# Same-chunk products of a gated scan, 64 x 64 in two column halves of the matmul array instead of 128 x 128

## The chip, the cores and the metric

The kernel runs on one core of a Trainium2 chip. The metric is the device time of one execution in microseconds (us). Besides it, a trace of one profiled execution is used; it shows every instruction of the five engines: TensorE (PE in the rows; its weight loads are PEld), VectorE (DVE), ScalarE (ACT), GpSimd (POOL) and SyncE (SP, which issues DMAs).

## What is computed

The reference is a two-layer backbone over 640 tokens (128 context tokens and 512 latent ones) of width 1024. A layer multiplies the modulated tokens by one wide input matrix, feeds four mixers (HGRN2, neighbourhood attention, MLA, short convolution), gates and projects their outputs, and ends in a layer norm. The change touches the HGRN2 mixer alone: four heads per layer, each a gated linear scan, forwards and backwards, in chunks.

```python
def step(S, inp):                       # one chunk
    qc, kc, vc, gc = inp
    b = jnp.cumsum(gc, axis=2)
    diff = b[:, :, :, None, :] - b[:, :, None, :, :]
    decay = jnp.exp(jnp.where(causal[:, :, None], diff, -jnp.inf))
    attn = jnp.einsum('bhtd,bhsd,bhtsd->bhts', qc, kc, decay)
    o = (jnp.einsum('bhts,bhse->bhte', attn, vc)
         + jnp.einsum('bhtd,bhde->bhte', qc * jnp.exp(b), S))
    ...
o_f, s_f = chunk_gla(q, heads(k_f, HG_DK), v, heads(lg_f, HG_DK), s0_f)
o_b, s_b = chunk_gla(rev(q), rev(heads(k_b, HG_DK)), rev(v), rev(heads(lg_b, HG_DK)), s0_b)
```

`attn` is the product of a query and a key under the decay between their positions. Every (query, key) pair has its own decay, so `attn` is not one plain matmul.

## The kernel before, in words

**The large work.** The input matrix comes as 128-column chunks. `zchunk` (line 237) takes one chunk's weights, which `take_w` (line 163) loads by DMA and splits in a high part `whi` (a cast on ACT, line 160) and a low part `wlo` (a subtraction on DVE, line 161), and multiplies them with the tokens' high and low parts in `zmm` (line 211): three matmuls for each of eight 128-row slices, for 384 tokens, and again for 256. These are the matmuls of line 217. The merges and the output use `mm3` (line 200, matmuls of line 208).

**The order of the work.** Each mixer is a generator. `tick` (line 141), called once before each half of a `zchunk`, lets every active generator go on by one step when its wait has run out. `hg_mix` (line 483) yields `HG_WAIT = 2` before each of its matmul groups, so about one group of HGRN matmuls stands between two halves of the large work. Within that, a scheduler orders each engine's instructions from the written order and from priorities; `take_w` asks for its load and split 300 places early. Each engine then runs its queue strictly in that order.

**The HGRN head.** `hg_mix` has the 640 tokens as five blocks `j` of 128. `RK` holds two copies of the keys, `RQ` two copies of the queries (forward and backward scan), channels on partitions. The products `A` (640 columns: for each `j`, 128 keys on partitions by 128 queries) are built in eight steps:

- the self product (line 501): five f32 matmuls of 128 keys by 128 queries, copied to `A` by ACT (line 503);
- seven levels, `B` = 1, 2, 4, ... 64. A level is the product of keys in one run of `B` positions with queries in the neighbouring run. ACT gathers the keys to `km` (line 511); five matmuls (line 516) read the queries through an access pattern that takes `B` elements from one copy of `RQ` and `B` from the other in turn; DVE writes the result to `A` where the level's mask is set (`copy_predicated`, line 519); then DVE multiplies the gates into `RK` and `RQ` for the next level (lines 524, 526, 528) and halves the gate products (line 530).

Most of what a level computes is masked away. Afterwards `A` is multiplied with the values (line 572), together with the states (lines 549, 562).

One f32 matmul of the program is two pairs of weight load (LDWEIGHTS) and MATMUL in the trace, so a group of five shows as x10. I call such a group a burst. Two layers of four heads with eight bursts each make 64.

Of the kernel before, what the change touches and what calls it, by code (L numbers as in the profile page):

```python
# [11 lines left out]
U8 = mybir.dt.uint8  # L12
# [6 lines left out]
T = 640  # L19
# [63 lines left out]
def ap_of(t, off, dims):  # L83
    base = t[:]
    return bass.AP(tensor=base.tensor, offset=base.offset + off, ap=[list(base.ap[0])] + [list(d) for d in dims])


class Build:
# [216 lines left out]

    def setup_tables(self):
        nc, I, cp = self.nc, self.I, self.cp
        mk = self.s([128, 7, 128])
        nc.scalar.dma_start(mk, I["masks"])
        self.masks = cp.tile([128, 7, 128], U8, name="masks")  # L310
        nc.vector.tensor_copy(self.masks, mk)
        self.cs = cp.tile([128, 2, 512], F32, name="cs")
        nc.scalar.dma_start(self.cs, I["cs"])
# [169 lines left out]
    def hg_mix(self, l, h, z, out):  # L483
        nc = self.nc
        G, RK, RQ, q, vT, sg = z
        S0 = self.u([128, 2, 128])
        nc.sync.dma_start(S0, self.I["S0"][l, h])
        ks = self.t()
        nc.vector.tensor_tensor(ks, RK[:, 0, :], RK[:, 1, :], ALU.add)
        yield HG_W0  # L490

        ps = self.mx()
        for j in range(5):
            nc.tensor.transpose(ps[:, j * 128:(j + 1) * 128], vT[:, j * 128:(j + 1) * 128], self.ident)
        v = self.t()
        nc.scalar.copy(v, ps[:, :T])

        ps = self.mx()
        for j in range(5):
            sl = slice(j * 128, (j + 1) * 128)  # L500
            nc.tensor.matmul(ps[:, sl], ks[:, sl], q[:, sl], start=True, stop=True)
        A = self.t()
        nc.scalar.copy(A, ps[:, :T])
        nc.vector.tensor_tensor(RQ[:, 0, :], q, G[:, 0, :], ALU.mult)
        nc.vector.tensor_tensor(RQ[:, 1, :], q, G[:, 1, :], ALU.mult)
        Tb, n = G, T
        for lev in range(7):
            B = 1 << lev
            np_ = T // (2 * B)
            km = self.t()  # L510
            nc.scalar.copy(km.rearrange("p (n u b) -> p n u b", u=2, b=B),
                           ap_of(RK, 0, [[2 * B, np_], [T + B, 2], [1, B]]))
            yield HG_WAIT
            ps = self.mx()
            for j in range(5):
                nc.tensor.matmul(ps[:, j * 128:(j + 1) * 128], km[:, j * 128:(j + 1) * 128],  # L516
                                 ap_of(RQ, j * 128, [[2 * B, 64 // B], [T + B, 2], [1, B]]),
                                 start=True, stop=True)
            nc.vector.copy_predicated(A.rearrange("p (j t) -> p j t", j=5),  # L519
                                      self.masks[:, lev:lev + 1, :].to_broadcast([128, 5, 128]),  # L520
                                      ps[:, :T].rearrange("p (j t) -> p j t", j=5))

            kf = ap_of(RK, 0, [[2 * B, np_], [1, B]])
            nc.vector.tensor_tensor(kf, kf, ap_of(Tb, n + 1, [[2, np_], [0, B]]), ALU.mult)
            kb = ap_of(RK, T + B, [[2 * B, np_], [1, B]])
            nc.vector.tensor_tensor(kb, kb, ap_of(Tb, 0, [[2, np_], [0, B]]), ALU.mult)
            rq = ap_of(RQ, 0, [[2 * B, np_], [T + B, 2], [1, B]])
            nc.vector.tensor_tensor(rq, rq, ap_of(Tb, 1, [[2, np_], [n - 1, 2], [0, B]]), ALU.mult)  # L528
            T2 = self.t([128, 2, np_]) if lev == 0 else self.u([128, 2, np_])
            nc.vector.tensor_tensor(T2, ap_of(Tb, 0, [[n, 2], [2, np_]]), ap_of(Tb, 1, [[n, 2], [2, np_]]), ALU.mult)  # L530
            Tb, n = T2, np_
        yield HG_WAIT

        order = ((0, 1, 2, 3), (0, 4, 3, 2))
        ps = self.mx()
        for d in range(2):
            for i, j in enumerate(order[d]):
                o = (4 * d + i) * 128
                nc.tensor.transpose(ps[:, o:o + 128], RK[:, d, j * 128:(j + 1) * 128], self.ident)
        kt = [self.t([128, 4, 128]) for _ in range(2)]  # L540
        for d in range(2):
            nc.scalar.copy(kt[d], ps[:, 512 * d:512 * d + 512].rearrange("p (i t) -> p i t", i=4))
        yield HG_WAIT
        vv = lambda j: v[:, j * 128:(j + 1) * 128]
        ps = self.mx()
        for d in range(2):
            for i, j in enumerate(order[d]):
                o = (4 * d + i) * 128
                nc.tensor.matmul(ps[:, o:o + 128], kt[d][:, i, :], vv(j), start=True, stop=True)  # L549
        st = self.u([128, 2, 128])  # L550
        nc.scalar.copy(st, ps.rearrange("p (d i t) -> p d i t", d=2, i=4)[:, :, 0, :])
        nc.sync.dma_start(self.O["state"][l, h], st)
        S = [self.u([128, 3, 128]) for _ in range(2)]
        terms = {j: [(A[:, j * 128:(j + 1) * 128], vv(j))] for j in range(5)}
        for d in range(2):
            prev = S0[:, d, :]
            for i in range(1, 5):
                j = order[d][i] if i < 4 else (4, 1)[d]
                terms[j].append((RQ[:, 1 - d, j * 128:(j + 1) * 128], prev))
                if i < 4:  # L560
                    o = (4 * d + i) * 128
                    nc.vector.scalar_tensor_tensor(S[d][:, i - 1, :], prev, Tb[:, 1 - d, j:j + 1], ps[:, o:o + 128],
                                                   ALU.mult, ALU.add)
                    prev = S[d][:, i - 1, :]
        yield HG_WAIT

        ps = self.mx()
        for j in range(5):
            if j == 3:
                yield 1  # L570
            for i, (a, b) in enumerate(terms[j]):
                nc.tensor.matmul(ps[:, j * 128:(j + 1) * 128], a, b, start=(i == 0), stop=(i == len(terms[j]) - 1))  # L572
        sq = self.t()
        nc.scalar.activation(sq, ps[:, :T], AF.Square)
        ss = self.sm([128, 5])
        nc.vector.tensor_reduce(ss, sq.rearrange("p (j e) -> p j e", j=5), AX.X, ALU.add)
        r = self.sm([128, 5])
        self.rsqrt(r, ss, 5, 1.0 / 128, EPS)
        on = sq
        nc.vector.tensor_tensor(on.rearrange("p (j e) -> p j e", j=5), ps[:, :T].rearrange("p (j e) -> p j e", j=5),  # L580
                                r.unsqueeze(2).to_broadcast([128, 5, 128]), ALU.mult)
        yield HG_WAIT
        ps = self.mx()
        for j in range(5):
            nc.tensor.transpose(ps[:, j * 128:(j + 1) * 128], on[:, j * 128:(j + 1) * 128], self.ident)
        nc.vector.scalar_tensor_tensor(sg, ps[:, :T], self.vec("normg", l), sg, ALU.mult, ALU.mult)
        out[h] = sg
# [478 lines left out]
    def out_norm(self, l, p):  # L1066
# [12 lines left out]
        for c in range(8):  # L1079
# [4 lines left out]
            if l + 1 < L:  # L1084
                for o, x, j in ((0, 128, 0), (128, n, 1)) if p == 0 else ((0, n, 1),):
                    A, B = self.hA[:, c, j:j + 1], self.hB[:, c, j:j + 1]
                    nc.scalar.activation(self.h_hi[:, c, a + o:a + x], y[:, o:x], AF.Identity, bias=B, scale=A)
                    if p == 0 and F_POOL:
                        nc.gpsimd.tensor_scalar(f[:, o:x], y[:, o:x], A, B, ALU.mult, ALU.add)
                    elif p == 1 and F_ACT:  # L1090
# [215 lines left out]
def _consts():  # L1306
    c = {}
    c["ident"] = np.eye(128, dtype=np.float32)
    s = np.arange(128)
    masks = np.zeros((128, 7, 128), np.float32)  # L1310
    for i in range(7):
        B = 1 << i
        blk = s // B
        same = (blk[:, None] // 2) == (blk[None, :] // 2)
        masks[:, i, :] = same & (blk[:, None] != blk[None, :])
    c["masks"] = masks
    t = np.arange(512)
    row, col = (t // 64).astype(np.float32), (t % 64).astype(np.float32)
    inv = (np.float32(1.0) / (np.float32(10000.0) ** (np.arange(16, dtype=np.float32) / np.float32(16)))).astype(np.float32)
    ang = np.concatenate([row[:, None] * inv, col[:, None] * inv], axis=-1).astype(np.float32)  # L1320
    cos, sin = np.cos(ang).astype(np.float32).T, np.sin(ang).astype(np.float32).T
    c["cs"] = np.stack([np.concatenate([cos] * 4, axis=0), np.concatenate([sin, -sin] * 2, axis=0)], axis=1)
    return c
# [90 lines left out]
```

## Time and profile before

| | |
|---|---|
| median of 3 runs | 2148.61 us (2146.55 to 2150.0) |
| the profiled execution, its own time | 2149.83 us |
| its span, first to last instruction | 2148.0 us |
| TensorE matmul, busy | 2095.0 us, 98% |
| VectorE, busy | 1378.0 us, 64% |
| ScalarE, busy | 867.1 us, 40% |
| granted TensorE clock, mean | 0.989 |

Busy times count an instruction from its start to its end, and on TensorE neighbouring instructions overlap: a matmul of 0.33 us can be followed by the next after 0.17 us. What a matmul takes away from its engine is therefore read from the distance between two starts, not from its own duration. A bracket at the end of a timeline row gives the idle time of the engine before it, and who ended it. The page's "chain" follows the work that ended last back to what released it.

### The profile page before, as it was taken

To read this page: it belongs to the slowest core of one execution; us is meant where nothing else is said; L and a number is where in the kernel's file an instruction comes from. 1 tells how busy PE (TensorE), PEld (TensorE's weight loads), DVE (VectorE), ACT (ScalarE), POOL (GpSimd) and SP (SyncE) were. 2 spreads that over 40 slices of the span, in tenths; PEclk is the share of its full clock that TensorE was granted. 3 is DMA by queue.
4 is the path that set the end of the run, shared out by engine and by line. 5 is a ranking of instruction groups with operands and counts; after the bars stand their busy time and mean duration, and the time that the engine had idled before them with its cause. 6 is when DMAs were issued, how large, how long until landed. Compare 5 with 4: busy or idle time off the path is not lost.

```text
span 2148.0 us, 35645 instructions
## 1 busy us (share of the span) xinstructions
PE 2095.0 (98%) x14538; PEld 2055.4 (96%) x14538; DVE 1378.0 (64%) x2648; ACT 867.1 (40%) x1531; POOL 179.1 (8%) x156
## 2 busy tenths in 40 slices
PE   7999999999999999999999999999999999999997
PEld 4999999998999999999999999999999999999997
DVE  5677776657666467734587876875575546775456
ACT  4333233344444466523352323343343336653332
POOL 0000000221111023200010000012000002221000
PEclk9999999999999999999999999999999999999998
DMA  7221222242222221122432222233221221222251
GB/s 281 78 63 61 65 67 70 86 132 77 93 96 93 67 68 62 60 74 74 148 116 72 62 62 65 62 101 91 61 75 61 60 67 59 71 66 60 75 166 50
DMA packets 70485, 178.05 MB, mean 83 GB/s; under 512 B 7985, under 2 KB 20913, under 8 KB 70321
## 3 DMA queue, kind: packets, MB, share of 16 engines
q1 hardware_dynamic: 67440, 169.32, 24.9%
q10 hardware_dynamic: 2880, 6.45, 0.9%
q8 instruction: 114, 1.87, 0.4%
q14 instruction: 51, 0.41, 0.1%
HBM read 168.20 MB, written 7.54 MB: 82 GB/s over the span
## 4 chain that ended last, share of the span: by engine, by line
PE 87%; DVE 7%; issue 2%; ACT 2%; DMA 2%; POOL 0%; SPq 0%; DVEq 0%; ACTq 0%; POOLq 0%
PE g L217 55%; PE g L208 13%; PE mx L516 3%; PE mx L756 2%; PE mx L971 2%; PE mx L208 1%; PE mx L794 1%; PE mx L217 1%; DVE wlo L161 1%; PE mx L938 1%; PE mx L572 1%; DVE t L161 1%; PE mx L770 1%; PE mx L549 1%; PE mx L394 1%
## 5 line engine op out<-in xcount | busy, mean ns | idle before, releaser
L217 PE MATMUL g<-h_hi,whi 128*128 128x256 f32 (+1 forms) x2880 | 905.2, 315 | 10.7 <-DVE e L1024 6.9
L217 PE MATMUL g<-h_lo,whi 128*128 128x256 f32 (+1 forms) x2880 | 893.5, 310 | 2.2 <-DVE h_lo L412 2.1
L217 PE MATMUL g<-h_hi,wlo 128*128 128x256 f32 (+1 forms) x2880 | 892.9, 310 | 0.6 <-DVE wlo L161 0.6
L217 PEld LDWEIGHTS g<-h_hi,whi 128*128 128x128 f32 x2880 | 548.1, 190 | 14.7 <-DVE e L1024 8.0
L217 PEld LDWEIGHTS g<-h_lo,whi 128*128 128x128 f32 x2880 | 549.0, 191 | 3.7 <-DVE h_lo L412 2.7
L217 PEld LDWEIGHTS g<-h_hi,wlo 128*128 128x128 f32 x2880 | 548.5, 190 | 1.0 <-DVE wlo L161 1.0
L161 DVE TENSOR_TENSOR wlo<-wraw,whi 128x1024 fp32r<-128x1024 f32 (+1 forms) x258 | 285.1, 1105 | 279.6 <-ACT whi L160 277.9
L160 ACT CAST whi<-wraw 128x1024 fp32r<-128x1024 f32 (+1 forms) x258 | 242.5, 940 | 478.4 <-PE g L217 261.0
L208 PE MATMUL g<-t,whi 128*128 128x256 f32 (+1 forms) x1280 | 284.7, 312 | 4.9 <-ACT e L1009 4.9
L208 PEld LDWEIGHTS g<-t,whi 128*128 128x128 f32 x1280 | 215.3, 190 | 6.2 <-ACT e L1009 5.7
L208 PE MATMUL g<-t,wlo 128*128 128x384 f32 (+1 forms) x640 | 198.3, 310 | 0.0
L387 POOL TENSOR_TENSOR t<-t 128x512 f32<-128x512 f32 x56 | 79.7, 1423 | 1017.0 <-ACT t L386 1016.0
L894 POOL TENSOR_SCALAR u<-u,sm 128x320 f32<-128x320 f32 (+2 forms) x80 | 89.9, 1135 | 569.7 <-DVE sm L892 532.9
L208 PEld LDWEIGHTS g<-t,wlo 128*128 128x128 f32 x640 | 121.5, 190 | 0.0
L1009 ACT ACTIVATE e<-g,hbin 128x384 f32<-128x384 f32 (+1 forms) x128 | 66.9, 523 | 116.0 <-PE g L217 115.9
L516 PE MATMUL mx<-s,t 128*128 128x128 f32 x560 | 76.4, 285 | 4.1 <-DVE s L528 4.1
L260 ACT ACTIVATE e<-g,hbin 128x384 f32<-128x384 f32 x76 | 39.8, 524 | 98.0 <-PE g L217 80.8
L516 PEld LDWEIGHTS mx<-s,t 128*128 128x128 f32 x560 | 72.8, 192 | 4.4 <-issue 4.4
L261 DVE TENSOR_SCALAR e<-g,vecs 128x384 f32<-128x384 f32 x76 | 41.4, 544 | 48.6 <-ACT e L260 48.4
L457 DVE RECIPROCAL s<-e 128x384 f32<-128x384 f32 (+1 forms) x32 | 68.9, 2152 | 0.9
L385 DVE SCALAR_TENSOR_TENSOR t<-t,cf 128x512 f32<-128x512 f32 x56 | 51.8, 925 | 20.5 <-DMA t<-in_wada 20.2
L519 DVE COPY_PREDICATED t<-masks,mx 128x640 f32<-128x640 uint8 x56 | 49.0, 876 | 23.8 <-PE mx L516 23.8
(282 smaller groups left out, 2672.1 us busy)
## 6 DMA issues: line engine op xcount, KB each, us to landing
wraw<-in_win SPq DMA_DIRECT2D x184, 512.0 KB, 3.5
wraw<-in_wbr SPq DMA_DIRECT2D x64, 256.0 KB, 2.6
t<-in_wada SPq DMA_DIRECT2D x64, 256.0 KB, 4.2
wraw<-in_wout SPq DMA_DIRECT2D x20, 512.0 KB, 4.4
s<-in_wada SPq DMA_DIRECT2D x16, 512.0 KB, 7.6
s<-in_nabias SPq DMA_DIRECT2D x8, 640.0 KB, 4.7
m<-in_xT SPq DMA_DIRECT2D x8, 320.0 KB, 8.4
t<-in_xT ACTq DMA_DIRECT2D x8, 320.0 KB, 5.0
```

The source lines that it names most:

```text
L160: nc.scalar.copy(hi, raw)
L161: nc.vector.tensor_tensor(lo, raw, hi.bitcast(F32), ALU.subtract)
L208: nc.tensor.matmul(o, wsl(a, k), xsl(b, k, i), start=(k == 0 and p == 0), stop=(k == nk - 1 and p == 2))
L217: nc.tensor.matmul(ps[:, :e - a], at(u, k), v[:, k, a:e], start=(k == 0 and i == 0), stop=(k == 7 and i == 2))
L385: nc.vector.scalar_tensor_tensor(acc[0], raw, cf(0), acc[0], ALU.mult, ALU.add)
L387: nc.gpsimd.tensor_tensor(acc[1], acc[1], raw, ALU.add)
L457: nc.vector.reciprocal(g, r)
L516: nc.tensor.matmul(ps[:, j * 128:(j + 1) * 128], km[:, j * 128:(j + 1) * 128], ap_of(RQ, j * 128, [[2 * B, 64 // B], [T + B, 2], [1, B]]), ...
L519: nc.vector.copy_predicated(A.rearrange("p (j t) -> p j t", j=5), self.masks[:, lev:lev + 1, :].to_broadcast([128, 5, 128]), ps[:, :T].rea ...
L756: nc.tensor.matmul(ps[:, e * 512:e * 512 + NH], a, b[:, e * NH:(e + 1) * NH], start=(n == 0), stop=(n == 4))
L894: NORM(nc).tensor_scalar(p[e], p[e], sums[:, e:e + 1], None, ALU.mult)
L1009: self.zchunk(l, "merge", n * 8 + c, lambda ps, p, sl: nc.scalar.activation(th[p], ps, AF.Tanh, bias=hb, scale=0.5))
```

## The change

The HGRN head no longer multiplies 128 keys by 128 queries. For the self product and the levels `B` = 1 to 32 it takes the 64 keys and 64 queries of each half-block, and puts the result of the first half on the output partitions 0 to 63 and that of the second half on 64 to 127; by this the weights of the first half lie in the columns 0 to 63 of the array and those of the second in 64 to 127. For `B` = 64 the keys of one half meet the queries of the other half. All results are compact: 64 columns for each `j`, 320 in all, in a tile `C` instead of `A`. The mask shrinks to 6 levels of 64 columns. At the last level ACT copies `C` and the last result to the four quadrants of `A` (four copies of 64 x 5 x 64 each head); that level has no `copy_predicated` any more.

```diff
-        mk = self.s([128, 7, 128])
+        mk = self.s([128, 6, 64])
...
+        halves = (slice(0, 64), slice(64, 128))
+        five = lambda x: x[:, 0:320].rearrange("p (j t) -> p j t", j=5)
         ps = self.mx()
         for j in range(5):
-            sl = slice(j * 128, (j + 1) * 128)
-            nc.tensor.matmul(ps[:, sl], ks[:, sl], q[:, sl], start=True, stop=True)
-        A = self.t()
-        nc.scalar.copy(A, ps[:, :T])
+            for i, r in enumerate(halves):
+                sl = slice(j * 128 + 64 * i, j * 128 + 64 * i + 64)
+                nc.tensor.matmul(ps[r, j * 64:(j + 1) * 64], ks[:, sl], q[:, sl], start=True, stop=True)
+        C = self.t([128, 5, 64])
+        nc.scalar.copy(C, five(ps))
...
             for j in range(5):
-                nc.tensor.matmul(ps[:, j * 128:(j + 1) * 128], km[:, j * 128:(j + 1) * 128],
-                                 ap_of(RQ, j * 128, [[2 * B, 64 // B], [T + B, 2], [1, B]]),
-                                 start=True, stop=True)
-            nc.vector.copy_predicated(A.rearrange("p (j t) -> p j t", j=5),
-                                      self.masks[:, lev:lev + 1, :].to_broadcast([128, 5, 128]),
-                                      ps[:, :T].rearrange("p (j t) -> p j t", j=5))
+                for i, r in enumerate(halves):
+                    o = j * 128 + 64 * i
+                    if B < 64:
+                        x = ap_of(RQ, o, [[2 * B, 32 // B], [T + B, 2], [1, B]])
+                    else:
+                        x = RQ[:, 1 - i, j * 128 + 64 - 64 * i:j * 128 + 128 - 64 * i]
+                    nc.tensor.matmul(ps[r, j * 64:(j + 1) * 64], km[:, o:o + 64], x, start=True, stop=True)
+            if B < 64:
+                nc.vector.copy_predicated(C, self.masks[:, lev:lev + 1, :].to_broadcast([128, 5, 64]), five(ps))
+            else:
+                A = self.t()
+                Aj = A.rearrange("p (j t) -> p j t", j=5)
+                for i, r in enumerate(halves):
+                    nc.scalar.copy(Aj[r, :, 64 * i:64 * i + 64], C[r])
+                    nc.scalar.copy(Aj[r, :, 64 - 64 * i:128 - 64 * i], five(ps)[r])
```

In the changed file the self product is line 506, the level matmul 527, `copy_predicated` 529, the four copies 535 and 536; the lines 524, 526 and 528 of before are 539, 541 and 543, and line 1022 is 1037.

**An ordinary burst.** TensorE's queue at the first self product (line 501, now 506), between the 384-token half and the 256-token half of a chunk; `mx` and `g` are PSUM tiles, `t` a tile in SBUF. Before:

```order
L217 MATMUL g<-h_hi,whi 128x384
L217 MATMUL g<-h_lo,whi 128x384
L217 MATMUL g<-h_hi,wlo 128x384
L501 MATMUL mx<-t 128x128 x5
L217 MATMUL g<-h_hi,whi 128x256
```

After:

```order
L217 MATMUL g<-h_hi,whi 128x384
L217 MATMUL g<-h_lo,whi 128x384
L217 MATMUL g<-h_hi,wlo 128x384
L506 MATMUL mx<-t 64x64 x10
L217 MATMUL g<-h_hi,whi 128x256
```

The burst stays where it was, with twice the matmuls of a quarter the size. This holds for all bursts but one in each layer.

**The burst that moves.** TensorE's queue at level `B` = 16 of the fourth head, in the first merge (line 208 is the merge's matmul). Before, two of the five matmuls stand right behind the merge's matmuls and three follow after 24 rows of line 217:

```order
L208 MATMUL g<-t,whi 128x256 x2
L208 MATMUL g<-t,wlo 128x256
L516 MATMUL mx<-s,t 128x128 x2
L217 MATMUL g<-h_hi,whi 128x384
L217 MATMUL g<-h_lo,whi 128x384
```

After, all ten stand behind those 24 rows:

```order
L217 MATMUL g<-h_hi,whi 128x384
L217 MATMUL g<-h_lo,whi 128x384
L217 MATMUL g<-h_hi,wlo 128x384
L527 MATMUL mx<-s,t 64x64 x10
L217 MATMUL g<-h_hi,whi 128x256
```

**VectorE at the same place.** Line 385 is part of the next modulation's sum, 161 makes `wlo`, 519 (now 529) is the masked copy and 528 (now 543) the query update that the burst waits for. Before:

```order
L385 SCALAR_TENSOR_TENSOR t<-t,cf 128x512
L526 TENSOR_TENSOR s<-s,u 128x5x64
L385 SCALAR_TENSOR_TENSOR t<-t,cf 128x512 x2
L161 TENSOR_TENSOR wlo<-wraw,whi 128x1024
L519 COPY_PREDICATED t<-masks,mx 128x640
L528 TENSOR_TENSOR s<-s,u 128x40x2x8
L1022 SCALAR_TENSOR_TENSOR m<-e,g 128x384
```

After:

```order
L385 SCALAR_TENSOR_TENSOR t<-t,cf 128x512
L541 TENSOR_TENSOR s<-s,u 128x5x64
L385 SCALAR_TENSOR_TENSOR t<-t,cf 128x512
L529 COPY_PREDICATED t<-masks,mx 128x320
L543 TENSOR_TENSOR s<-s,u 128x40x2x8
L161 TENSOR_TENSOR wlo<-wraw,whi 128x1024
L1037 SCALAR_TENSOR_TENSOR m<-e,g 128x384
```

The masked copy and the query update now stand ahead of `wlo` and of one row of line 385.

## Rows read from the trace of the kernel before

**Rows 1.** The page, part 1: busy time, share of the span, instructions.

```profile
PE 2095.0 (98%) x14538; PEld 2055.4 (96%) x14538; DVE 1378.0 (64%) x2648; ACT 867.1 (40%) x1531; POOL 179.1 (8%) x156
```

**Rows 2.** The page, part 4: the chain that ended last, by engine.

```profile
PE 87%; DVE 7%; issue 2%; ACT 2%; DMA 2%; POOL 0%; SPq 0%; DVEq 0%; ACTq 0%; POOLq 0%
```

**Rows 3.** HGRN windows: length; busy PE, PEld, DVE, ACT, POOL; PEclk, DMA share, GB/s.

```profile
119.00:427.00 308.00, 304.68 (x2187) 304.04 (x2186) 222.52 (x377) 104.34 (x156) 10.86 (x7) 1.00 0.22 69
1170.00:1480.00 310.00, 306.67 (x2190) 306.00 (x2188) 230.84 (x397) 105.63 (x158) 10.87 (x7) 0.99 0.22 69
```

**Rows 4.** Groups by line and shape: count, busy us, mean ns, idle before.

```profile
L516 PE MATMUL mx<-s,t 128*128 128x128 f32 x560 | 76.4, 285 | 4.1 <-DVE s L528 4.1
L501 PE MATMUL mx<-t 128*128 128x128 f32 x80 | 10.2, 275 | 0.0
```

**Rows 5.** Timeline, weight loads around three bursts: start, us, engine, line.

```profile
128.08 1.69 PEld L516 LDWEIGHTS mx<-s,t 128*128 128x128 f32 x10
129.74 0.20 PEld L217 LDWEIGHTS g<-h_hi,whi 128*128 128x128 f32 x1
...
136.77 1.32 PEld L516 LDWEIGHTS mx<-s,t 128*128 128x128 f32 x10
138.02 0.19 PEld L217 LDWEIGHTS g<-h_hi,whi 128*128 128x128 f32 x1
...
144.83 0.19 PEld L217 LDWEIGHTS g<-h_hi,wlo 128*128 128x128 f32 x1
145.01 1.25 PEld L516 LDWEIGHTS mx<-s,t 128*128 128x128 f32 x10
146.18 0.19 PEld L217 LDWEIGHTS g<-h_hi,whi 128*128 128x128 f32 x1
```

**Rows 6.** Timeline, weight loads: full f32 weights, 2 moving columns each.

```profile
420.60 1.87 PEld L394 LDWEIGHTS mx<-ones,t 128*128 128x128 f32 x16
422.38 0.30 PEld L208 LDWEIGHTS g<-t,whi 128*128 128x128 f32 x2
```

**Rows 7.** Timeline, weight loads: four short pairs on one tile of the array.

```profile
18.13 0.32 PEld L359 LDWEIGHTS mx<-ident,t 4*128 4x128 f32 x4 [0.86 <-issue]
```

**Rows 8.** Timeline, weight loads: f32 matmuls over halves of the array's rows.

```profile
794.91 0.19 PEld L217 LDWEIGHTS g<-h_lo,whi 128*128 128x128 f32 x1
795.03 0.19 PEld L217 LDWEIGHTS g<-h_hi,wlo 128*128 128x128 f32 x1
795.35 0.30 PEld L903 LDWEIGHTS mx<-u,t 64*128 64x128 f32 x4
795.77 0.19 PEld L217 LDWEIGHTS g<-h_hi,whi 128*128 128x128 f32 x1
```

**Rows 9.** Timeline, weight loads: to and from matmuls with 4 weight columns.

```profile
32.89 0.19 PEld L217 LDWEIGHTS mx<-h_hi,t 128*128 128x128 f32 x1
33.01 0.43 PEld L352 LDWEIGHTS mx<-t,c 128*4 128x4 f32 x3
...
38.33 0.09 PEld L352 LDWEIGHTS mx<-t,c 128*4 128x4 f32 x1
38.56 0.41 PEld L217 LDWEIGHTS g<-h_hi,whi 128*128 128x128 f32 x2
```

**Rows 10.** Timeline, matmuls: the moved burst in each layer.

```profile
399.68 0.68 PE L516 MATMUL mx<-s,t 128*128 128x128 f32 x4 [2.02 <-DVE s L528]
...
1456.68 0.68 PE L516 MATMUL mx<-s,t 128*128 128x128 f32 x4 [2.04 <-DVE s L528]
```

**Rows 11.** Windows behind the second of these: the columns of rows 3.

```profile
1457.30:1460.60 3.30, 3.30 (x12) 3.30 (x11) 0.92 (x2) 0.00 (x0) 0.37 (x1) 0.50 0.37 117
1461.00:1464.00 3.00, 3.00 (x23) 3.00 (x22) 0.19 (x1) 0.58 (x1) 0.00 (x0) 1.00 0.01 4
```

**Rows 12.** Groups by line and shape, VectorE and ScalarE.

```profile
L519 DVE COPY_PREDICATED t<-masks,mx 128x640 f32<-128x640 uint8 x56 | 49.0, 876 | 23.8 <-PE mx L516 23.8
L503 ACT COPY t<-mx 128x640 f32<-128x640 f32 x8 | 5.6, 696 | 3.0 <-PE mx L501 3.0
```

More of the change, by code (lines that the diff above doesn't have):

```diff
@@ L307, in setup_tables @@
         nc, I, cp = self.nc, self.I, self.cp
-        mk = self.s([128, 7, 128])
+        mk = self.s([128, 6, 64])
         nc.scalar.dma_start(mk, I["masks"])
-        self.masks = cp.tile([128, 7, 128], U8, name="masks")
+        self.masks = cp.tile([128, 6, 64], U8, name="masks")
         nc.vector.tensor_copy(self.masks, mk)
@@ L1308, in _consts @@
     c["ident"] = np.eye(128, dtype=np.float32)
[L1309 to L1315, printed above, removed]
+    s, t = np.arange(128) % 64, np.arange(64)
+    masks = np.zeros((128, 6, 64), np.float32)
+    for i in range(6):
+        a, b = s // (1 << i), t // (1 << i)
+        masks[:, i, :] = (a[:, None] // 2 == b[None, :] // 2) & (a[:, None] != b[None, :])
     c["masks"] = masks
```

## The prediction

> **What bounds the kernel now.** First the page's busy times: TensorE is busy for 98% of the span, VectorE for 64%, ScalarE for 40% [rows 1]. Then the chain of waits, which asks what the end hangs on: 87% of it is TensorE [rows 2]. Both are averages, so I look at the stages that the change touches. The eight HGRN heads run in two windows of 308 and 310 us, and TensorE has work for 304.7 and 306.7 us of them [rows 3]. VectorE has 222.5 and 230.8 us there, ScalarE a third. So in these windows nearly every us that TensorE saves should end the kernel earlier, and every us that another engine saves is worth nothing while TensorE is the slower one.
>
> How much of TensorE do these products take? The self products are 80 pairs of weight load and matmul, the levels 560 [rows 4]. Their busy time (76.4 and 10.2 us) merges overlapping instructions; what they really occupy is read from starts. At level `B` = 4 the first of ten loads starts at 145.01, the next foreign one at 146.18: 1.17 us [rows 5]. The first of the ten gaps in it belongs to the 384-token matmul ahead, which holds the engine for some 0.17 us (its load starts at 144.83); the other nine make 1.00, so one pair of the burst costs 0.111 us. In the same way `B` = 2 gives 1.25 us, 0.120 a pair, and `B` = 1, where the query pattern jumps at every element, 1.66 us, 0.165 a pair [rows 5]. The self product and `B` = 4 to 64 are 48 bursts, `B` = 2 and `B` = 1 eight each: 48 x 1.11 + 8 x 1.20 + 8 x 1.65 = 76 us, 3.5% of the span. That is all there is to win.
>
> What holds a pair at 0.111 us? Sixteen pairs with full weights and only 2 moving columns take 420.60 to 422.38, again 0.111 us each [rows 6]. So loading 128 f32 weight columns already costs it, and fewer moving columns alone would win nothing.
>
> **The change, part by part.**
>
> *The halved bursts.* A burst has 20 pairs instead of 10, each with half the weight columns and half the moving columns. By itself that is no gain: 1280 weight columns and 1280 moving columns as before. It pays only if the two halves of the array load and multiply at the same time. No row shows column halves doing that. The nearest is a pair of f32 matmuls over halves of the array's rows: its four loads lie within 0.30 us, the last one 0.11 after the first, where four full ones would take 4 x 0.111 [rows 8]. There two halves do work at once. I take it that column halves do so too, because it is the same kind of instruction on the same array; that is the uncertain step.
>
> The price of one half pair lies between half of 0.111, 0.056 us, and the shortest steady spacing on one tile that I find, four short pairs within 0.32 us where the last load lasts 0.14, so 0.061 each [rows 7]. I take 0.061, the measured one. Ten deep (two halves side by side): 0.61 us for 48 bursts, 0.61 for the eight at `B` = 2 (half of 0.120 is 0.060), and half of 0.165, 0.083, for the eight at `B` = 1, where the pattern sets the pace. Gain: 48 x 0.50 + 8 x 0.59 + 8 x 0.82 = 24.0 + 4.7 + 6.6 = 35.3 us. With 0.056 it would be 38.0.
>
> *Entering and leaving the half form.* The row halves show a cost: the load before them starts 0.12 after its neighbour, the first half load 0.32 after that, and from the first half load to the next full one 0.42 us pass where two rounds of 0.11 would do; 0.20 us on each side [rows 8]. Matmuls with 4 weight columns, a column form too, show none: their load follows the full one after 0.12 us, and the full one follows theirs after 0.23, which is just their 512 moving columns [rows 9]. The bounds are therefore 0 and 0.40 us a visit; there are 60 visits in the new order (four times two bursts stand together), so 0 to 24 us. Columns are nearer to columns: I take 0. The Trainium skill (TensorEngine Tiling (Array Packing), Key Properties) states the opposite: a change of tiling mode drains the array. The row halves agree with it, by 0.20 us a side; the 4-column matmuls do not; by that rule the sum would be some 24 us higher.
>
> *The moved burst.* TensorE stands still for 2.02 and 2.04 us before the fourth head's `B` = 16 burst, waiting for the query update [rows 10]. After the second wait the clock is granted at 0.50, the 1.2 GHz level, for 3.3 us, and is back at 1.00 behind it [rows 11]: half of that, 1.6 us, is lost. In the new order the burst stands behind 24 matmuls (24 x 0.17 = 4.2 us), and the update stands ahead of `wlo` and of one partial sum, so this wait goes. What is late next is `wlo`, now behind the masked copy and the update; the third matmul of those 24 needs it. Bounds: 0 and 2.02 + 2.04 + 1.6 = 5.7 us gained; I take 2, since VectorE is nearly full there and TensorE arrives earlier.
>
> *VectorE and ScalarE.* 48 masked copies of 320 columns take the place of 56 of 640 at 0.876 us [rows 12]: at least 7 us less on VectorE, hidden behind TensorE. ScalarE gets 32 copies of 64 x 320, each between 0.35 and 0.70 us (half of and all of the 640-column copy), and loses half of eight: 8 to 20 us more over the whole run on an engine that idles 60% of it [rows 1, 12]. Two of each four wait for the last level's burst, and weight casts queue behind them; but in TensorE's queue that burst stands ahead of the matmuls that need these casts. I cost both at nothing; the cover is the third of each window in which VectorE and ScalarE wait. The smaller mask load and its cast happen once, below 1 us. SyncE moves one weight load ahead of an initial state and one modulation load behind two weight loads; DMA is at 0.22 [rows 3], so nothing.
>
> **Sum.** Against the profiled execution's 2149.8 us (span 2148.0): 2149.8 - 35.3 - 2 = 2112.5, rounded to 2112 us. The median of the runs shown, 2148.6, is 0.06% lower, and I don't correct for it. A measurement of this kernel can tell about 0.2%, 4.3 us, from no change.
>
> **The rivals.**
>
> *Overlap, but a drain on every visit.* The 60 visits pay 0.40 us: 2112 + 24 = 2136. For it: the row halves [rows 8]. Against: the 4-column form [rows 9]. 12%.
>
> *The halves queue.* If weight loads for two column halves take turns, a burst is 20 x 0.056 to 20 x 0.061 = 1.11 to 1.22 us, against 1.11: no gain, up to 6 lost, 2 won at the moved burst: 2148 to 2154. For it: both halves read the same 128 partitions, unlike the row halves, and the load is what holds a pair. Against: nothing in the trace, since loads of different tiles of one row group never stand side by side in it. The Trainium skill (TensorE: Matmul & The Clock Gate, Part 3, "What overlaps and what doesn't") states a rule that leads here: weight loads overlap running matmuls only where the row group differs. The trace does not agree for the large work, where full loads recorded at 0.19 us start every 0.12 in the same rows [rows 8]. 13%, about 2149.
>
> *Slower: they queue, and every visit drains.* Twenty loads in turn save nothing and 60 x 0.40 = 24 us come on top: 2149.8 + 24 - 2 = 2172. It decides as soon as the overlap saves less than the 0.40 us that a visit costs; full overlap saves 0.50. For it: the two rows that speak for its halves [rows 6, 8]. Against: the 4-column form again. 17%.
>
> **How the numbers follow.** Overlap without a drain gets 58%, for the row halves that visibly work at once and the column form that visibly does not drain. With 12, 13 and 17% for the rivals: faster by over 0.2%: 58 + 12 = 70%; within 0.2% (2145.5 to 2154.1): 12%; slower: 17 and the last of the queueing case, 18%. The range: the low end is the best price with the whole stall, 2149.8 - 38.0 - 5.7 = 2106, less 2 us, by which the fastest run shown lies below the median: 2104. The high end takes in the drain and most of the queueing case: 2152. That holds 58 + 12 + about 11, some 81%.
>
> **What would show it.** Right: the distance from a burst's first load to the next foreign one falls from 1.17 to about 0.65 us at `B` = 4 and from 1.66 to about 0.9 at `B` = 1; loads of the new lines start in pairs a few ns apart; the loads on either side keep their 0.12 to 0.17; the idle time before the fourth head's `B` = 16 burst is gone. Wrong: 20 single loads 0.056 to 0.061 apart (they queue); 0.2 us holes at the edges (they drain); or the bursts halve and the span does not, with idle TensorE before line 217 and VectorE or ScalarE named as its releaser.

## The result, and the profile after

The changed kernel takes 2132.36 us (median of 4 runs, 2130.3 to 2136.42) against 2148.97 us of the kernel before (4 runs, 2146.55 to 2150.0): ratio 0.9928, 95% interval 0.9915 to 0.994, 16.6 us less. The forecast was 2112 us, 36.6 below the median then known. The profiled execution took 2130.3 us, with a span of 2128.5. One run of a probe below, probe_half_high, took 2946.68 us at a mean granted clock of 0.651; it is left out, and because its trace is of that run, that probe is read by its times alone.

The page after: the span, part 1 and part 4, beside [rows 1, 2]:

```profile
span 2128.5 us, 36950 instructions
PE 2075.1 (97%) x15178; PEld 2019.5 (95%) x15178; DVE 1357.5 (64%) x2640; ACT 878.8 (41%) x1563; POOL 178.8 (8%) x156
...
PE 29%; DVE 2%; ACT 0%; issue 0%; POOL 0%; DVEq 0%; ACTq 0%; POOLq 0%
```

TensorE is still the engine that is always busy. The chain breaks off after a third of the span here, so its shares can't be set against [rows 2]; what there is of it is again TensorE.

The HGRN stage of each layer, from the first self product's load to the first load of line 394. The columns are those of [rows 3]. Before:

```profile
119.93:420.60 300.67, 297.35 (x2134) 296.71 (x2134) 217.14 (x366) 103.23 (x154) 10.86 (x7) 1.00 0.22 70
1176.93:1479.15 302.22, 298.89 (x2135) 298.25 (x2133) 223.55 (x388) 103.29 (x154) 10.87 (x7) 0.99 0.23 69
```

After:

```profile
118.42:411.67 293.25, 290.78 (x2454) 281.73 (x2453) 206.06 (x363) 108.19 (x168) 10.70 (x7) 0.99 0.23 71
1166.95:1459.72 292.77, 290.54 (x2453) 281.84 (x2453) 212.79 (x385) 108.01 (x168) 10.70 (x7) 0.99 0.24 71
```

The two stages are 7.4 and 9.5 us shorter: 16.9 of the 19.5 us by which the spans differ. So the gain came where it was looked for, but more than half of the forecast is missing there.

One burst shows why. Timeline of the weight loads around level `B` = 4 after; the counterpart is the third piece of [rows 5]:

```profile
142.18 0.19 PEld L217 LDWEIGHTS g<-h_hi,wlo 128*128 128x128 f32 x1
142.62 0.66 PEld L527 LDWEIGHTS mx<-s,t 128*64 128x64 f32 x20 [0.25 <-issue]
143.35 0.19 PEld L217 LDWEIGHTS g<-h_hi,whi 128*128 128x128 f32 x1
143.46 0.19 PEld L217 LDWEIGHTS g<-h_lo,whi 128*128 128x128 f32 x1
```

The same loads of line 527 in slices of 0.06 us (busy time and count of the loads that touch the slice, then clock, DMA share, GB/s):

```profile
142.60:142.66 0.06, 0.04 (x2) 1.00 0.50 205
142.66:142.72 0.06, 0.06 (x4) 1.00 0.34 137
142.72:142.78 0.06, 0.06 (x6) 1.00 0.89 341
142.78:142.84 0.06, 0.06 (x6) 1.00 0.17 68
```

Two more loads stand in each slice until the first ones end: the halves load side by side, in rounds of two. From the first of the twenty to the next foreign load it is 0.73 us, where the ten full ones took 1.17. But 0.44 us pass from the last full load to the first half load, against 0.18 before ([rows 5]: 144.83 to 145.01); the row shows 0.25 of it as idle time with nothing waited for. From the last full load ahead to the second one behind, a visit (one stay in the half form, between full loads) took 1.46 us before (144.83 to 146.18, and 0.11 on) and takes 1.28 now (142.18 to 143.46): 0.18 gained, not 0.50.

### The profile page after: what moved, and what is told of

The parts are those of the page before. It is cut to its first block, busy times and chain, and to the rows that moved or that the text cites. A ratio compares the mean times of both kernels' runs of the same rounds, so it can differ in the third digit from the quotient of the medians.

```text
span 2128.5 us, 36950 instructions
## 1 busy us (share of the span) xinstructions
PE 2075.1 (97%) x15178; PEld 2019.5 (95%) x15178; DVE 1357.5 (64%) x2640; ACT 878.8 (41%) x1563; POOL 178.8 (8%) x156
## 5 line engine op out<-in xcount | busy, mean ns | idle before, releaser
L386 ACT ACTIVATE t<-t,cf 128x512 f32<-128x512 f32 x56 | 40.0, 720 | 45.8 <-DVE t L385 35.6
L834 ACT ACTIVATE t<-mx,sm,rq 128x640 f32<-128x640 f32 (+1 forms) x40 | 31.8, 796 | 55.7 <-DVE sm L831 51.9
L1039 DVE SCALAR_TENSOR_TENSOR e<-e,g 128x384 f32<-128x384 f32 x96 | 46.5, 484 | 12.7 <-PE g L208 12.0
```

Of the source, the lines that this page charges most:

```text
L386: nc.scalar.activation(raw, raw, AF.Copy, scale=cf(1))
L1039: nc.vector.scalar_tensor_tensor(th[p], th[p], 1.0, ps, ALU.add, ALU.mult)
```

## The experiments

The theory after the result: the halves overlap as forecast, and each change between full and half columns drains the array, some 0.40 us a visit, 24 us in 60 visits; the trace would show this as holes, longer distances between the loads at both edges. Rivals: the holes belong to the second half's place, or to two halves side by side; the halves disturb each other inside the burst; the new order of VectorE and ScalarE costs what is missing. All ratios below are to the kernel before, run on the same chip, with 95% intervals; the times of the kernel before differ a little from chip to chip.

**Four probes in the kernel before.** Each of the 56 level bursts gets one matmul more behind its five, into columns 640 to 703 of the tile, which nobody reads:

```diff
+            nc.tensor.matmul(ps[:, 640:704], km[:, 0:128], q[:, 0:64], start=True, stop=True)         # probe_full
+            nc.tensor.matmul(ps[0:64, 640:704], km[:, 0:64], q[:, 0:64], start=True, stop=True)       # probe_half_low
+            nc.tensor.matmul(ps[64:128, 640:704], km[:, 64:128], q[:, 0:64], start=True, stop=True)   # probe_half_high
+            nc.tensor.matmul(ps[0:4, 640:704], km[:, 0:4], q[:, 0:64], start=True, stop=True)         # probe_four
```

> The kernel before, with one f32 matmul more at the end of each of the 56 level bursts, over all 128 weight columns and 64 moving columns, into 64 columns of the tile that nobody reads. This is the control: one pair of load and matmul at 0.111 us, 56 x 0.11 = 6 us, so about 2155 us. No theory expects a hole at the edges.

> The kernel before, with one extra f32 matmul per level burst as in the control, but over 64 weight columns in array columns 0 to 63, into columns that nobody reads. Theory (each change between full and half columns drains the array, some 0.2 us a side): 56 x (0.40 + 0.11) = 29 us, about 2177 us, and the trace shows 0.2 us holes on both sides of the extra load. Rival (the loss in the changed kernel comes not from the form but from the second half, or from two halves side by side): 56 x 0.06 to 0.12 = 3 to 7 us, 2152 to 2156 us, no holes.

> The same extra matmul over 64 weight columns, but in array columns 64 to 127 (PSUM partitions 64 to 127). Theory (the form drains, wherever it lies): 29 us as for columns 0 to 63, about 2177 us. Rival (only the half that does not start at column 0 drains): 29 us here and 3 to 7 us there. Rival (neither alone drains): 2152 to 2156 us.

> The same extra matmul over only 4 weight columns in array columns 0 to 3. This is the form of the rows that showed no drain, but with f32 operands and 64 moving columns. If a few columns at the array's edge never drain: 56 x 0.06 to 0.11 = 3 to 6 us, 2152 to 2155 us. If the earlier rows hid a drain behind their 512 moving columns: 29 us, about 2177 us.

Measured: probe_full 2159.89 us (ratio 1.0046, 1.0031 to 1.0061), probe_half_low 2173.21 (1.0115, 1.01 to 1.013), probe_half_high 2173.68 (1.0113, 1.0096 to 1.013), probe_four 2169.85 (1.0096, 1.0081 to 1.0111); before 2149.42. The control came out at 10.5 us and not 6: an f32 matmul is two pairs of load and matmul, and its expectation counted one (56 x 0.224 = 12.5). A half costs 24 us more than before wherever it lies, over twice the control, and even four columns cost 20.

Weight loads around one such matmul of probe_half_low:

```profile
142.47 1.25 PEld L516 LDWEIGHTS mx<-s,t 128*128 128x128 f32 x10
143.85 0.19 PEld L519 LDWEIGHTS mx<-t 128*64 128x64 f32 x2
144.10 0.19 PEld L217 LDWEIGHTS g<-h_hi,whi 128*128 128x128 f32 x1
144.21 0.19 PEld L217 LDWEIGHTS g<-h_lo,whi 128*128 128x128 f32 x1
```

and of probe_four:

```profile
144.50 1.25 PEld L516 LDWEIGHTS mx<-s,t 128*128 128x128 f32 x10
145.87 0.09 PEld L519 LDWEIGHTS mx<-t 128*4 128x4 f32 x2
146.07 0.19 PEld L217 LDWEIGHTS g<-h_hi,whi 128*128 128x128 f32 x1
146.18 0.19 PEld L217 LDWEIGHTS g<-h_lo,whi 128*128 128x128 f32 x1
```

The last full load ends at 142.47 + 1.25 = 143.72 and started 0.19 earlier, at 143.53; the half load follows at 143.85, 0.31 to 0.32 later instead of 0.11. In the median over the 56 bursts of each probe, from the single starts, it is 0.313 us in both. Behind the matmul the next full load follows the second half load after 0.203 us in the one and 0.200 in the other; inside the half form a load follows the last after 0.055. So a visit costs 0.313 - 0.112 = 0.20 us going in and 0.20 - 0.055 = 0.15 coming out, 0.35 in all. Four columns have the same two holes; their two loads start only 0.005 us apart, which makes them cheaper by 56 x 0.05 = 3 us. A single half drains, on either side of the array (columns 64 to 127 by the time alone); the rivals of place and of two halves side by side fall. But [rows 9] showed four columns without a hole, and probe_four has one.

**What spares the rows of before.** The 4-column matmuls of [rows 9] have float32r operands and one pair of load and matmul each; the probes have f32 and two. Two more probes take the layer input's float32r tile as operands:

```diff
+            nc.tensor.matmul(ps[0:64, 640:704], self.h_hi[:, 0, 0:64], self.h_hi[:, 0, 64:128], start=True, stop=True)  # probe_half_f32r
+            nc.tensor.matmul(ps[0:4, 640:704], self.h_hi[:, 0, 0:4], self.h_hi[:, 0, 64:128], start=True, stop=True)    # probe_four_f32r
```

> The kernel before, with one extra matmul per level burst over 64 weight columns in array columns 0 to 63 as in probe_half_low, but with float32r operands (one pair of load and matmul instead of two), like the 4-column matmuls of the kernel before that showed no hole. Theory A (what spares those is the operand type): no holes, 56 x 0.06 to 0.12 = 3 to 7 us, 2152 to 2156 us. Theory B (what spares them is the width or the neighbours, the type does nothing): holes of 0.20 us on each side as in probe_half_low, 56 x (0.40 + 0.06) less the 0.11 or so that overlaps, 20 to 26 us, 2169 to 2175 us.

> The same extra float32r matmul over only 4 weight columns: the very form of the 4-column matmuls of the kernel before, except for 64 moving columns in place of 512 and f32 matmuls ahead. Theory A (operand type): no holes, 2151 to 2155 us. Theory B: holes of 0.20 us a side as in probe_four, about 2169 us; then the rows before hid them in some way of their own.

Measured: 2154.28 us (1.0031, 1.002 to 1.0043) and 2156.03 (1.004, 1.0025 to 1.0055); before 2147.65. That is 6.6 and 8.4 us where the f32 forms cost 24 and 20. Loads of probe_half_f32r (the first row is nine of the ten, the view merges them at its left edge):

```profile
141.91 1.08 PEld L516 LDWEIGHTS mx<-s,t 128*128 128x128 f32 x9
142.91 0.14 PEld L519 LDWEIGHTS mx<-h_hi 128*64 128x64 f32 x1
143.02 0.19 PEld L217 LDWEIGHTS g<-h_hi,whi 128*128 128x128 f32 x1
143.13 0.19 PEld L217 LDWEIGHTS g<-h_lo,whi 128*128 128x128 f32 x1
```

0.11 us in and 0.11 out: no hole. In the median over the 56 bursts it is 0.112 and 0.111, in probe_four_f32r too. Theory A fits, though probe_four_f32r lies 1 us above its range. The kernel before has two more rows that bear on it. Transposes of 64 columns (line 868; f32, one pair each; the row's five include two of 64 columns) run at 0.11 a pair, with no hole ahead or behind, and a float32r product over half of the array's rows (line 971) follows its neighbour after 0.32:

```profile
791.63 0.14 PEld L866 LDWEIGHTS mx<-ident,t 128*128 128x128 f32 x1
791.73 0.55 PEld L868 LDWEIGHTS mx<-ident,t 128*64 128x64 f32 x5
792.28 0.19 PEld L217 LDWEIGHTS g<-h_hi,whi 128*128 128x128 f32 x1
...
772.67 0.19 PEld L217 LDWEIGHTS g<-h_hi,wlo 128*128 128x128 f32 x1
772.99 0.84 PEld L971 LDWEIGHTS mx<-s,t 64*128 64x128 f32 x5
```

So in these runs fewer columns drain the array in two-pair f32 matmuls and not in one-pair ones, and fewer rows drain it in both. Operand type and number of pairs changed together in the probes, so which of the two spares them is not shown, nor why; the transposes, f32 with one pair, speak for the number of pairs. The float32r probes lie at column 0, and two float32r halves side by side were not run.

**Is anything lost inside the burst?** The changed kernel with each level burst issued twice, and the changed kernel with both halves in the same columns (the self product likewise, and the copies read partitions 0 to 63 alone):

```diff
-            for j in range(5):
+            for j in [0, 1, 2, 3, 4] * 2:                                   # after_twice
```

```diff
-                    nc.tensor.matmul(ps[r, j * 64:(j + 1) * 64], km[:, o:o + 64], x, start=True, stop=True)
+                    nc.tensor.matmul(ps[0:64, 320 * i + j * 64:320 * i + (j + 1) * 64], km[:, o:o + 64], x, start=True, stop=True)   # after_one_side
```

> The changed kernel with the twenty matmul pairs of each of the 56 level bursts issued twice in a row, same results. The second set needs no change of form, so it costs what the halves cost when the array is in their form. Theory (halves overlap fully, the loss is all at the edges): 10 rounds of 0.057 us, 0.57 us a burst (0.85 at B = 1), 56 bursts 34 us, about 2167 us. Rival (the halves disturb each other and the loss is inside the burst): 0.97 us a burst, 54 us, about 2187 us.

> The changed kernel, but the products of both halves of queries and keys use array columns 0 to 63, one after the other, into different columns of PSUM. Since the second half's results then lie on the wrong partitions, only half of the scores is used (the output is not the reference's). The form and the number of visits stay, the side-by-side work goes. Theory (the halves do work at once in the changed kernel): 20 turns of 0.055 to 0.061 in place of 10 rounds of 0.057, 64 x 0.57 = 36 us (0.57 to 0.64 a burst), about 2168 us. Rival (they take turns already, in loads that only start in pairs): no difference, about 2132 us.

Measured: after_twice 2167.52 us (1.0094, 1.0079 to 1.0109), 35 us over the changed kernel; after_one_side 2172.45 (1.0113, 1.01 to 1.0127), 40 over it. A `B` = 4 burst of after_twice:

```profile
143.75 1.25 PEld L527 LDWEIGHTS mx<-s,t 128*64 128x64 f32 x40 [0.25 <-issue]
145.07 0.19 PEld L217 LDWEIGHTS g<-h_hi,whi 128*128 128x128 f32 x1
```

and of after_one_side:

```profile
145.31 1.24 PEld L528 LDWEIGHTS mx<-s,t 128*64 128x64 f32 x20 [0.25 <-issue]
146.61 0.19 PEld L217 LDWEIGHTS g<-h_hi,whi 128*128 128x128 f32 x1
```

Twenty loads more side by side cost 1.32 - 0.73 = 0.59 us, 0.058 a round of two; twenty loads in one half of the array take 1.30, as long as forty in two. The halves work at once without loss, and nothing is missing inside the burst. The 0.25 us of idle time ahead of it is the same in all three.

**What the change does off TensorE.** The changed kernel with the full products of before; only their first 64 columns are read:

```diff
-                for i, r in enumerate(halves):
...
+                nc.tensor.matmul(ps[:, j * 128:(j + 1) * 128], km[:, j * 128:(j + 1) * 128],
+                                 ap_of(RQ, j * 128, [[2 * B, 64 // B], [T + B, 2], [1, B]]),
+                                 start=True, stop=True)
```

> The changed kernel, except that the level and self products run as the full 128 by 128 matmuls of the kernel before; copies, masks, ScalarE's placing copies and the order of everything else stay as in the changed kernel. Only the first 64 columns of each product are read, so the second half of the scores is left out of the output. It prices what the change does off TensorE. Theory (that is worth next to nothing): 2145 to 2151 us. Rival (the order of VectorE and ScalarE costs the missing gain): well above, up to 2149 + 18 = 2167 us. Rival (the moved burst's 2 us come, as forecast): about 2147 us.

Measured: 2151.05 us, ratio 1.0015 (1.0006 to 1.0024): 3.2 us slower than before, 1.3 to 5.2, where the forecast had 2 gained. The waits of TensorE from 385 to 412 us, before:

```profile
PE mx L516 <- DVE s L528: 2.0, 1, 2.0
PE g L208 <- ACT e L1009: 1.3, 1, 1.3
```

and in full_other_after:

```profile
PE g L217 <- DVE m L1032: 2.4, 1, 2.4
PE g L208 <- ACT e L1019: 1.3, 1, 1.3
```

The burst no longer waits. In its place line 217, which needs the tile that VectorE's `m` frees, waits 0.4 us longer than the burst did, and behind it the clock falls below 1.00 in both layers (windows of 2 us from 396 and from 1458 us), before only in the second. The longer waits are 2 x 0.4 of the 3.2 us. In these two traces the one more fall of the clock, half of 3.4 us, would make it 2.5; but the clock falls there in some traces and not in others, as the next section shows, so the rest of the 3.2 us stays open.

**Fewer visits.** If a fixed price a visit is what is lost, products that stand together give it back. A group of products fills one PSUM tile; for every level but the last of a group ScalarE gathers a copy of the queries, so that the update can run ahead of the products:

```diff
+HG_GROUPS = ((-1, 0), (1, 2), (3, 4), (5, 6))      # merged_two; merged_three: ((-1, 0, 1), (2, 3, 4), (5, 6)); -1 is the self product
...
+                if lev != group[-1]:
+                    qs[lev] = gather(RQ, B)
+                    update(lev)
+            ps = self.mx()
+            for m, lev in enumerate(group):
...
+                        c = 320 * m + j * 64
+                        nc.tensor.matmul(ps[r, c:c + 64], keys[lev][:, o:o + 64], x, start=True, stop=True)
```

> The changed kernel with two products in one visit: self with B = 1, 2 with 4, 8 with 16, 32 with 64, 32 visits in place of 60. For the first of two levels ScalarE gathers a copy of the queries ahead of the update, 24 copies of 640 columns more. Theory (what is lost is 0.40 us a visit): 28 x 0.40 = 11 us less than the changed kernel's 2132, about 2121 us, ratio 0.987. Rival (the edges' holes are hidden by something else, or the loss goes with the number of products): 2132 us or more.

> The same with groups of three: self, 1 and 2; 4, 8 and 16; 32 and 64: at least 24 visits (some are split where the order of matmuls puts others between). Theory: up to 36 x 0.40 = 14 us below the changed kernel, 2118 to 2121 us, unless the longer chain of VectorE and ScalarE work ahead of each visit makes TensorE wait. Rival: as for two.

Measured: merged_two 2123.25 us (0.9884, 0.9871 to 0.9898), 9.1 below the changed kernel for 28 visits fewer, 0.33 a visit. merged_three 2115.76 us (0.9844, 0.9831 to 0.9858), 16.6 below it, with 29 visits (the order of matmuls splits some groups). It is the fastest of all eleven variants. By visits alone, 31 x 0.35 = 11 us, it would be 2121.5. Two more things differ in its trace. The `B` = 1 products read a gathered copy of the queries, and their rounds fall from 0.085 to 0.058 us: the self product and `B` = 1 together start 131.49 - 130.33 = 1.16 us ahead of `B` = 2, twenty rounds of 0.058, which is 8 x 10 x 0.027 = 2 us in all (in merged_two `B` = 1 still reads with the jumping pattern):

```profile
130.33 1.25 PEld L550 LDWEIGHTS mx<-t 128*64 128x64 f32 x40 [0.25 <-issue]
131.49 0.70 PEld L550 LDWEIGHTS mx<-s,t 128*64 128x64 f32 x20
```

And the stalls of the next section are nearly gone: TensorE's waits on lines 208 and 217 there are 0.4 us a layer (2.47 and 2.23 in the changed kernel), and the clock stays at 1.00. The wait of each layer (350 to 405 us and 1395 to 1445 us give the same line), then windows in either layer:

```profile
PE g L217 <- DVE m L1054: 0.4, 1, 0.4
```

```profile
370.00:380.00 10.00, 9.64 (x68) 9.43 (x67) 6.10 (x8) 5.19 (x8) 4.52 (x3) 1.00 0.35 111
...
1420.00:1430.00 10.00, 9.63 (x101) 9.11 (x99) 6.06 (x11) 3.18 (x5) 3.06 (x2) 1.00 0.52 159
```

Both parts were read from the trace and not tried by themselves.

## Why the prediction was right and wrong

**The halves overlap: right.** The term went by [rows 7, 8] and took 0.061 us for a half pair, ten deep. after_twice gives 0.058, and at `B` = 1 and 2 (1.83 - 0.98)/10 = 0.085 and (1.40 - 0.78)/10 = 0.061 against 0.083 and 0.060, from the starts of the forty and twenty loads. Two rivals fall with it: "the halves queue" and the slower one, queueing with a drain. The Trainium skill's rule in TensorE: Matmul & The Clock Gate, Part 3 (weight loads overlap running matmuls only where the row group differs) does not hold for them: their loads run from 142.62 to 143.28 us over the same 128 rows as their matmuls, which are recorded as running meanwhile, and the two loads of a round begin 6 to 7 ns apart:

```profile
142.62 0.80 PE L527 MATMUL mx<-s,t 128*64 128x64 f32 x20
```

after_one_side shows what it costs when the loads of the two halves take turns.

**The visit costs nothing: wrong, and this is the step that failed.** The prediction had both bounds, 0 and 0.40 us, from [rows 9] and [rows 8], and chose by likeness: "Columns are nearer to columns: I take 0". The likeness that mattered was another. Line 903 of [rows 8] is f32 with two loads a matmul, as the new products are; line 352 of [rows 9] is float32r with one. probe_four and probe_four_f32r differ in that and in the tiles they read, and one has the hole and the other hasn't. The operand type stood in the code; the trace prints both as f32, but line 903 has two loads for each matmul. Measured, a visit costs 0.35 us: 0.20 and 0.15 at the probes, and in the changed kernel 1.28 - (1.46 - 10 x 0.053) = 0.35, where 0.053 is what the side-by-side work saves of 0.111 a pair. 60 visits make 21 us. That is the rival "overlap, but a drain on every visit": 2136 us forecast for it, 2132.4 measured, at a chance of 12%. The Trainium skill (TensorEngine Tiling (Array Packing), Key Properties) states that a change of tiling mode drains the array. For f32 halves the runs agree, by 0.31 us in place of 0.11 going in; for float32r in 64 or 4 columns they show no drain.

**The moved burst: the wait went, the gain of 2 us is not shown.** The wait of [rows 10] went, as forecast, and something was late next, as forecast, but not `wlo`. It is the activation of line 1024, 1009 before. The prediction left it out, although TensorE waited 1.30 us for it before as well, some 3.7 us ahead of the burst. Timeline of TensorE at that place after, in the first layer and the second:

```profile
385.30 0.34 PE L208 MATMUL g<-t,wlo 128*128 128x384 f32 x1
388.11 0.51 PE L208 MATMUL g<-t,whi 128*128 128x256 f32 x2 [2.47 <-ACT e L1024]
388.45 0.28 PE L208 MATMUL g<-t,wlo 128*128 128x256 f32 x1
...
1436.30 0.56 PE L208 MATMUL g<-t,whi 128*128 128x256 f32 x2 [2.23 <-ACT e L1024]
```

and ScalarE's in the first:

```profile
386.03 0.72 ACT L386 ACTIVATE t<-t,cf 128x512 f32<-128x512 f32 x1 [1.22 <-DVE t L385]
386.66 1.03 ACT L160 CAST whi<-wraw 128x1024 fp32r<-128x1024 f32 x1
387.59 0.47 ACT L1024 ACTIVATE e<-g,hbin 128x256 f32<-128x256 f32 x1
```

The activation waits behind a cast, that behind line 386, that for VectorE's line 385. From line 386 to the activation it is 1.56 us, as before; TensorE gets there earlier with its shorter bursts and waits longer. In full_other_after, which has the order of the change and the long bursts, it waits 1.3 us here, as before, and the 2.4 us for `m` behind it. In the changed kernel TensorE waits 2.47 and 2.23 us in the two layers, where it waited 1.30 + 2.02 and 1.30 + 2.04 before: 2.0 us less in all. But in this trace the clock falls behind the wait in both layers, where [rows 11] showed it in the second alone:

```profile
388.60:392.00 3.40, 3.40 (x16) 3.15 (x15) 3.40 (x6) 0.97 (x3) 2.33 (x1) 0.52 0.26 74
1436.50:1439.90 3.40, 3.40 (x16) 3.38 (x16) 3.40 (x5) 0.98 (x2) 2.33 (x1) 0.52 0.19 36
```

Granted 0.52, the 1.2 GHz level nearly throughout, each costs half of 3.4 us, 1.7, once more than before, which leaves next to nothing of the 2.0. That fall can't be put down to the change: behind waits of 2.0 us at the same burst the clock stays at 1.00 in both layers of probe_full and falls to 0.50 in both of probe_half_low, and in after_twice, with waits of 2.2 us, it stays at 1.00 in both. So what the new order is worth is known only from full_other_after, 3.2 us lost with the long bursts.

**VectorE and ScalarE at nothing: right, but for that place.** The masked copies take 518 ns instead of 876 [rows 12], the placing copies 457 and 420 ns, inside the bounds of 0.35 to 0.70 us. Outside the stretch of the moved burst no wait of TensorE shows it: one of 1.81 us (line 217, at 512.22) is 3.28 after, but it has either value in probes of the kernel before too (1.77 in probe_full, 3.28 in probe_four).

**The sum anew.** 35.3 us, 1.9 more for rounds of 0.058 in place of 0.061 (64 x 10 x 0.003), less 21 for the visits, and for the order between 2.0 won (the waits of the trace) and 3.2 lost (full_other_after): 13 to 18 us gained, against 16.6 measured (12.9 to 18.3 by the ratio's interval). The drain is as large as the missing 20; the order is the open end, within some 5 us.

## What to carry to other kernels

Two column halves of the array do work at once in f32, at 0.058 us for two half pairs where a full one takes 0.111, but 0.35 us go with every change to that form and back, so it wants long visits: ten rounds a visit saved 0.18 us, and standing products together saved the price of each visit that fell away. When the price of a new form must be taken from the nearest rows, look at operand type and at the number of load and matmul pairs before the shape. And when a wait is ended by moving the waiting work, price what is late next, and look for waits that stand ahead of it already.

## What was not expected of the hardware

A narrow f32 matmul costs nearly as much as one over half of the array: one more matmul over 4 weight columns and 64 moving ones cost 20 us in 56 places, twice the full 128-column one (10.5 us), while the same in float32r cost 8.4. And fewer columns without a hole in a one-pair matmul stand beside fewer rows with one (line 971, 0.32 us): the two kinds of half are not alike.
